# A steep-decay branch among plain units, an early load of lambda's vectors, urgent closing additions and filler ahead of the first decay

## The chip, the cores and the metric

The kernel runs on one NeuronCore of a Trainium2 chip. The metric is the device time of one execution in microseconds (us). Engine names in this text: PE is TensorE (matmuls), PEld its weight loads, DVE is VectorE, ACT is ScalarE, POOL is GpSimd, SP is SyncE, which here issues all DMAs. A "q" behind an engine's name means its instruction queue (waits, branches, register loads).

## The reference

The reference is a two-layer decoder trunk on 512 tokens of width 1024 with 16 learned meta tokens in front (528 rows). The first layer is gated linear attention in four heads with chunked decay, the second differential attention in eight heads; each has an RMSNorm before it, a SiLU gate, and a residual addition after its output projection. Cut to what matters here:

```python
def gla_branch(xn, w_in, w_gate_up, b_gate, gnorm, w_out):
    q, k, v, z, g_lr = split(xn @ w_in)
    lg = log_sigmoid(g_lr @ w_gate_up + b_gate) / GLA_TAU      # the decay's logarithm
    # per chunk, b = cumsum(lg):
    #   attn_ij = sum_d q_id k_jd exp(b_id - b_jd), j <= i
    #   o = attn v + (q exp(b)) S ;  S = exp(b_last) S + (k exp(b_last - b))^T v
    o = head_rms(o) * gnorm
    return (silu(z) * o) @ w_out

def diff_branch(xn, w_in, lam_vecs, ...):
    lv = lam_vecs                                              # four vectors of 128
    lam = exp(sum(lv[0] * lv[1])) - exp(sum(lv[2] * lv[3])) + lambda_init
    # a = softmax(q0 k0 + bias) - lam * softmax(q1 k1 + bias)
```

## The kernel before, in words

Every float32 product is made of three matmuls of split operands: a high part (rounded copy, on ACT) and a low part (the remainder, on DVE), made by `split` (L235). Activations of the first layer are held transposed in four blocks of 4 x 128 rows by 264 columns (`X`, L466).

The first layer's projections are queued as generators in a `Weaver` (class at L73, object `W`). `W.fill(us)` takes steps from the queue's head until the given sum of nominal costs is used up; `W.finish(gen)` runs the queue until that generator is done, `W.settle()` also runs what was deferred. So the order of PE's instructions is written out by the order of these calls in the source, and it is kept as written (`manual_schedule` for PE, L190). For the other engines a scheduler orders instructions at compile time from priorities, which follow the program's order, and its own estimate of when inputs are ready; `urgent` (L227) raises the priority of what a function issues. A `tc.If` block is kept together as one piece.

There are two kinds of projection unit, each 256 columns of weights wide:

- a plain unit (`plain_unit`, L713): two halves, each with two PSUM banks taken by `pb_pair` (alternately the pair bx, bx and the pair bv, by), 48 matmuls a half, 16 steps in all, each of 6 matmuls and a nominal 0.66 us. After a half, `evac` reads the banks out. The value projections and the q and k projections of head 0 are plain units.
- a `Unit` (L360): a Strassen-like scheme of seven products of 12 matmuls, each product four steps of 3 matmuls and a nominal 0.33 us. Its closing additions are in `add` (L393): they read a bank (`by`, `bv` or `bx`) and a partial sum on DVE, at L398, L400 or L402; the bank is free for PE's next product after that. `tail` (L685) multiplies finished q or k rows by their decay factor (L687). The z projections of head 0, and all projections of heads 1 to 3, are such units: two in head 0 and six in each other head.

The order around the change is this. The low-rank gate projection runs on PE with five plain steps between (L817 to L823) and is read out of its two banks (bx, bx) to `gs` (L827 to L831). Three transposes of raw input follow (L840). Then eight decays: `decay(k)` (L845) is two matmuls from `gs` (L849), three ACT steps (L850 to L852), two DVE steps (L855) and a scan along the tokens (L856) into `b_all`; after each, `W.fill(3.5)`. After the eighth, a flag is made on DVE (L871, L872): whether any chunk's decay is so steep that factors would overflow. PE sums it over partitions (L1095), DVE casts it to an integer `fi` (L1096), every engine loads it to a register (L1098) and branches (L1099) around a long block that treats steep decay; with these inputs the block is skipped. Before this branch the queue is run to the end of head 0's last plain unit (L1090), and 1.0 and 3.0 us of the first z unit follow.

Per head there then come `gla_scores` (L973), `gla_ready` (L1021) and `gla_blocks` (L1028), with filler between. At head 1, `second_layer_setup` (L883) makes the second layer's bias rows and lambda: it loads the four vectors broadcast to all partitions (L896, 256 KB), multiplies and sums them on DVE (L897, L899), and takes exponents on ACT (L900). Constants are loaded by SP at the start (L494 to L526); every DMA goes through SP's one queue in its order.

## Time and profile before

| what | value |
|---|---|
| median of 3 runs | 1049.13 us (1047.19 to 1050.68) |
| the profiled execution's own time | 1049.57 us |
| its span, first to last instruction | 1047.8 us |
| mean granted clock of PE | 0.991 |
| PE busy, 490 to 1048 us (second layer and the end) | 548.75 of 558.00 us |
| PE busy, 86 to 100 us (around the branch) | 10.36 of 14.00 us, clock 0.76 |
| DVE busy, 100 to 490 us (heads 0 to 3) | 287.15 of 390.00 us |

The span is what the profile shows; the device time has 1.8 us around it. Busy times are those of one execution. PE's rows in the order of time overlap: a matmul's shown duration is longer than the distance to the next, so costs are taken from the distance. A wait is given as the idle time in front of an instruction, with what ended it behind an arrow.

### The profile page before, as it was taken

How to read it: one execution, taken by the hardware profiler on the slowest of the kernel's cores; microseconds unless marked ns; L12 is line 12 of the kernel's file. 1: busy time of each engine (PE TensorE's matmuls, PEld its weight loads, DVE VectorE, ACT ScalarE, POOL GpSimd, SP SyncE). 2: the span in 40 equal slices, each digit the busy share in tenths (PEclk: the TensorE clock that was granted, in tenths of full speed). 3: DMA queues.
4: the chain of work that ended last, by engine and by line, in shares of the span. 5: the costliest groups of instructions: out<-in, count | busy, mean ns of one | idle time of the engine just before them, and what ended most of it. 6: DMA issues, size and time to landing. Idle time of an engine off the chain costs nothing.

```text
span 1047.8 us, 18311 instructions
## 1 busy us (share of the span) xinstructions
PE 1017.8 (97%) x7345; PEld 954.0 (91%) x7345; DVE 718.8 (69%) x1441; ACT 544.5 (52%) x1198; POOL 37.9 (4%) x68
## 2 busy tenths in 40 slices
PE   8897999999999999999999999999999999999997
PEld 7897998998899999999999898998989989889995
DVE  7886886778767887564557675755757548576675
ACT  6773764356534656536435454444544445454453
POOL 1000000000000000000000000000000000000001
PEclk9998999999999999999999999999999999999999
DMA  7222312333223312222322122232222322222212
GB/s 197 67 60 66 84 44 90 81 81 82 81 59 92 93 43 79 82 81 86 117 82 91 51 82 81 81 92 81 81 91 82 90 82 59 83 72 82 80 41 81
DMA packets 98940, 84.56 MB, mean 81 GB/s; under 512 B 5517, under 2 KB 87725, under 8 KB 98848
## 3 DMA queue, kind: packets, MB, share of 16 engines
q1 hardware_dynamic: 98848, 83.31, 26.7%
q8 instruction: 60, 0.98, 0.4%
q14 instruction: 32, 0.26, 0.1%
HBM read 83.90 MB, written 2.12 MB: 82 GB/s over the span
## 4 chain that ended last, share of the span: by engine, by line
PE 77%; DVE 7%; ACT 2%; issue 2%; DMA 2%; POOL 1%; SPq 0%; POOLq 0%; DVEq 0%; ACTq 0%
PE pp L346 32%; PE ps L325 8%; PE pp L325 7%; PE bx L355 6%; PE bx L799 4%; PE bv L355 4%; PE by L355 3%; PE bv L799 2%; PE by L799 2%; PE ps L1010 2%; PE ps L710 1%; DMA raw<-in_gla_w_in_dram 1%; DVE wl L239 1%; PE ps L1337 1%; POOL st L457 1%
## 5 line engine op out<-in xcount | busy, mean ns | idle before, releaser
L346 PE MATMUL pp<-x,wh 128*128 128x264 f32 (+1 forms) x1504 | 321.7, 323 | 0.0
L346 PEld LDWEIGHTS pp<-x,wh 128*128 128x128 f32 x1504 | 227.0, 188 | 15.5
L238 ACT ACTIVATE wh<-raw 128x512 fp32r<-128x512 f32 (+1 forms) x212 | 138.1, 680 | 119.3 <-PE pp L346 52.6
L346 PE MATMUL pp<-x,wl 128*128 128x264 f32 (+1 forms) x752 | 198.2, 319 | 0.0
L239 DVE TENSOR_TENSOR wl<-raw,wh 128x512 fp32r<-128x512 f32 (+1 forms) x212 | 156.2, 757 | 43.3 <-ACT wh L238 42.1
L346 PEld LDWEIGHTS pp<-x,wl 128*128 128x128 f32 x752 | 124.3, 188 | 10.5
L457 POOL TENSOR_TENSOR st<-st,mhalf 128x1 f32<-128x1 f32 (+1 forms) x52 | 31.1, 597 | 932.7 <-DVE st L456 932.7
L1325 ACT ACTIVATE p<-p,st 128x528 f32<-128x528 f32 (+3 forms) x64 | 36.4, 569 | 49.4 <-DVE st L1324 49.0
L325 PE MATMUL pp<-wh,x 128*128 128x256 f32 x320 | 61.3, 282 | 0.0
L355 PE MATMUL bv<-x,wh 128*128 128x264 f32 x320 | 48.5, 289 | 3.6 <-DVE t L398 1.8
L325 PEld LDWEIGHTS pp<-wh,x 128*128 128x128 f32 x320 | 51.0, 189 | 0.1
L355 PE MATMUL bx<-x,wh 128*128 128x264 f32 x320 | 48.7, 292 | 0.0
L355 PEld LDWEIGHTS bv<-x,wh 128*128 128x128 f32 x320 | 42.4, 188 | 4.9 <-DVE ks L400 2.5
L325 PE MATMUL pp<-wl,x 128*128 128x256 f32 x160 | 45.1, 282 | 0.0
L355 PEld LDWEIGHTS bx<-x,wh 128*128 128x128 f32 x320 | 43.5, 193 | 0.7 <-issue 0.6
L1322 DVE SCALAR_TENSOR_TENSOR p<-ps,qr,T 128x264 f32<-128x264 f32 (+3 forms) x80 | 36.5, 490 | 6.4 <-PE ps L325 6.4
L374 ACT ACTIVATE u<-bx 128x264 f32<-128x264 f32 x60 | 22.9, 382 | 33.1 <-PE bx L355 31.2
L239 DVE TENSOR_TENSOR aT<-ps,aT 128x512 fp32r<-128x512 f32 (+3 forms) x32 | 15.7, 489 | 31.8 <-ACT aT L238 31.6
L325 PE MATMUL ps<-k,q 128*128 128x264 f32 (+3 forms) x240 | 36.8, 294 | 0.0
L325 PEld LDWEIGHTS ps<-k,q 128*128 128x128 f32 x240 | 33.6, 188 | 0.9
L239 DVE TENSOR_TENSOR wl<-sum,wh 128x1024 fp32r<-128x1024 f32 x20 | 24.4, 1221 | 14.5 <-ACT wh L238 9.6
L325 PE MATMUL ps<-v,aT 128*128 128x256 f32 x240 | 33.9, 282 | 0.0
(399 smaller groups left out, 2209.2 us busy)
## 6 DMA issues: line engine op xcount, KB each, us to landing
raw<-in_diff_w_in_dram SPq DMA_DIRECT2D x32, 1024.0 KB
raw<-in_gla_w_in_dram SPq DMA_DIRECT2D x48, 512.0 KB
raw<-in_gla_w_out_dram SPq DMA_DIRECT2D x8, 1024.0 KB
raw<-in_diff_w_out_dram SPq DMA_DIRECT2D x8, 1024.0 KB
T<-bdr SPq DMA_DIRECT2D x8, 264.0 KB
out_dram<-z SPq DMA_DIRECT2D x8, 256.0 KB
kd<-steep SPq DMA_DIRECT2D x4, 400.0 KB
t<-steep SPq DMA_DIRECT2D x4, 264.0 KB
```

What stands on the lines that cost most here:

```text
L238: act.activation(hi, src, AF.Copy)
L239: dve.tensor_tensor(lo, src, hi.bitcast(F32), op=ALU.subtract)
L325: pe.matmul(ps, l, r, start=first and n == 0, stop=last and n == 2, **kw)
L346: pe.matmul(bank, a[:, k, :], b[k][:, n0 + i * nn:n0 + (i + 1) * nn], start=k == 0 and n == 0, stop=k == nk - 1 and n == 2)
L355: pe.matmul(bank[:, :HT], w[p][:, k * P:(k + 1) * P], x[q][:, k, :], start=first and i == 0, stop=i == len(PASSES) - 1, skip_group_check=n ...
L374: act.activation(t, self.bx[:, :HT], AF.Copy, scale=self.sc)
L457: pool.tensor_tensor(dst, dst, mhalf[:np_, :dst.shape[1]], op=ALU.pow)
L710: pe.transpose(pt[:, b * P:(b + 1) * P], vt[:, t0:t0 + n], ident)
L799: pe.matmul(banks[i][:, :HT], h.t[p][:, k, mm * P:(mm + 1) * P], s.y[q][k][:, i * HT:(i + 1) * HT], start=n == 0, stop=n == len(PASSES) - 1)
L1010: pe.matmul(o, s.kd[:, i, kc], s.qs[:, i, t0:t0 + n], start=i == 0, stop=i == 1)
L1322: dve.scalar_tensor_tensor(p[:, c0:c1], ps[:, :c1 - c0], qr[:, b:b + 1], s.T[:, c0:c1], op0=ALU.mult, op1=ALU.add)
L1325: act.activation(p[:, :nk], p[:, :nk], AF.Exp, bias=st[:, m:m + 1], accum_out=st[:, 2 + m:3 + m])
```

## The change

There are five edits.

1. The additions in `add` and the multiplication in `tail` are made `urgent`.
2. Lambda's four vectors are loaded with the first constants, transposed to one column each (512 single elements, `lv`); in `second_layer_setup` their products are two columns (`lt`), which a matmul with a matrix of ones sums over the partitions in place of the broadcast load and DVE's reduction.
3. `W.fill(4.0)` stands before the first decay; the fill after decay 0 is 2.0 in place of 3.5.
4. The flag's matmul, the branch and its fills move ahead of `W.finish(first[-1])`, `token_sums(5)` and `W.settle()`, and the second fill is 1.5 in place of 3.0. Between decay 7 and the branch PE now takes plain steps: six, two, the flag's matmul, and three; one step of the last plain unit is left behind the branch.
5. At head 1, `W.fill(4.0)` comes after `second_layer_setup` as well, not only at the other heads.

```diff
@@ -390,6 +390,7 @@
+            @urgent
             def add(i, n, bank, t, sign):
@@ -524,6 +525,9 @@
+    lv = cp.tile([P, 4], F32, name="lv")
+    with nc.allow_non_contiguous_dma(reason="four short vectors"):
+        sp.dma_start(lv, d_lam.rearrange("a p -> p a"))
     act.preload_act_table_set("natural_log_exp_and_others")
@@ -682,6 +686,7 @@
             if hd:
+                @urgent
                 def tail(i, j=j, sign=sign):
@@ -858,9 +863,10 @@
     for half in range(2):
         q_gla_z(0, heads[0], half, raw=True)
+    W.fill(4.0)
     for k in range(KT):
         decay(k)
-        W.fill(3.5)
+        W.fill(3.5 if k else 2.0)
         if 1 <= k <= 5:
             token_sums(k - 1)
@@ -892,11 +898,12 @@
-        lamb, lt = tmp()[:, :4 * P].rearrange("p (a b) -> p a b", a=4), tmp()[:, :2 * P].rearrange("p (a b) -> p a b", a=2)
-        sp.dma_start(lamb, d_lam.partition_broadcast(P))
-        dve.tensor_tensor(lt, lamb[:, 0::2, :], lamb[:, 1::2, :], op=ALU.mult)
+        lt = T(cp, [P, 2], F32, "lt")
+        dve.tensor_tensor(lt, lv[:, 0::2], lv[:, 1::2], op=ALU.mult)
+        ps = ps_tile()
+        pe.matmul(ps[:, :2], ones, lt, start=True, stop=True)
         lam2 = T(cp, [P, 2], F32, "lam2")
-        dve.tensor_reduce(lam2, lt, axis=AX.X, op=ALU.add)
+        dve.tensor_copy(lam2, ps[:, :2])
         act.activation(lam2, lam2, AF.Exp)
@@ -1087,14 +1094,11 @@
-    W.finish(first[-1])
-    token_sums(5)
-    W.settle()
     W.fill(1.0)
     pf = ps_tile()
     pe.matmul(pf[0:1, 0:1], fl[:, 1:2], one1, start=True, stop=True)
     dve.tensor_copy(fi, pf[0:1, 0:1])
-    W.fill(3.0)
+    W.fill(1.5)
     steep = nc.values_load(fi[0:1, 0:1], min_val=0, max_val=P)
     with tc.If(steep > 0):
@@ -1102,6 +1106,9 @@
         sp.dma_start(hT, hT_dr)
+    W.finish(first[-1])
+    token_sums(5)
+    W.settle()
     for hd in range(G_HEADS):
@@ -1114,8 +1121,7 @@
             if hd == 1:
                 second_layer_setup()
-            else:
-                W.fill(4.0)
+            W.fill(4.0)
```

## The prediction

> **What bounds the kernel now.** I read the page first, then who TensorE (PE) waited for, then the granted clock by stretches, then the order of time around each wait.

> ```profile
> span 1047.8 us, 18311 instructions
> PE 1017.8 (97%) x7345; PEld 954.0 (91%) x7345; DVE 718.8 (69%) x1441; ACT 544.5 (52%) x1198; POOL 37.9 (4%) x68
> ```

> PE is the bound: it is idle for 1047.8 - 1017.8 = 30.0 us, so no change of order can bring more than those 30 us, and what PE loses to a lowered clock. The list of PE's waits (total, times, longest) says where the idle time is:

> ```profile
> PE bv L355 <- PEq L1099: 3.6, 1, 3.6
> PE bv L355 <- DVE t L398: 1.8, 1, 1.8
> PE ps L849 <- DVE a L831: 1.7, 1, 1.7
> PE bv L355 <- DVE ks L400: 1.7, 2, 0.9
> PE bx L355 <- DVE ks L698: 1.6, 1, 1.6
> PE ps L849 <- ACT hT L565: 0.7, 1, 0.7
> PE by L355 <- DVE t L398: 0.4, 1, 0.4
> ```

> All seven lie in the first layer, and each is touched by one edit: L1099 is the branch on `steep`, L849 the first decay, the wait of 1.8 stands behind lambda's load, L698 is the closing of the last plain unit, and L400 and the last L398 are additions in `add`. Together 11.5 us. The second cost shows in the busy times by stretches (the column PEclk is the granted clock):

> ```profile
> core 0: us, PE busy (x) PEld busy (x) DVE busy (x) ACT busy (x) POOL busy (x), PEclk, DMA share, GB/s
> 35.00:38.40 3.40, 3.40 (x18) 3.40 (x17) 3.40 (x7) 2.82 (x6) 0.00 (x0) 0.50 0.00 0
> 93.00:99.80 6.80, 5.45 (x26) 5.21 (x27) 2.48 (x5) 0.39 (x1) 0.00 (x0) 0.50 0.03 8
> 168.10:171.50 3.40, 3.40 (x18) 2.94 (x17) 2.12 (x5) 2.40 (x5) 0.00 (x0) 0.50 0.00 0
> ```

> After each of the three larger stalls PE runs at half clock: 3.40, 5.45 and 3.40 us of work, of which half is lost, so 1.7, 2.7 and 1.7 us on top of the waits. (The start-up, ahead of the change, has one more such stretch.) The unit of all that follows is one matmul of 264 columns, from the chain of waits:

> ```profile
> 103.92 1.46 PE bv L355 x12
> ```

> 1.46 / 12 = 0.122 us. A step of a plain unit is 6 of them (0.73 us, counted as 0.66 by the filler), a step of a `Unit` 3 (0.37 us, counted as 0.33).

> **The change part by part. First decay.**

> ```profile
> 30.76 0.66 PE L559 MATMUL ps<-ident,v 128*128 128x128 f32 x4 [0.39 <-ACT hT L565]
> 33.72 0.42 DVE L831 TENSOR_TENSOR a<-bx,a 16x264 fp32r<-16x264 f32 x1
> 34.20 0.39 PE L849 MATMUL ps<-a,z 128*128 128x264 f32 x1 [1.72 <-DVE a L831]
> ```

> PE ends the transposes at 31.42 and then has only the first decay, whose input DVE finishes at 34.14 (33.72 + 0.42): 0.7 and 1.7 us of waiting, 2.4 in all. `W.fill(4.0)` issues seven plain steps there (six count 3.96, not yet 4.0), 5.1 us, so PE arrives at 36.5 and finds everything ready: -2.4. One thing can come late: five steps were issued before, so the fourth of the seven begins the value unit's second half, in the bank pair that the gate projection's evacuation (L831) still reads. PE gets there at 31.4 + 3 x 0.73 = 33.6, up to 0.6 before 34.2. I take -2.2 (-2.4 to -1.8). The half clock of 35.0 to 38.4 goes with the gap: -1.7 (-1.7 to 0, if the clock falls elsewhere). The smaller fill after decay 0 (four steps for six) means that all later decays stand at about their old times, and PE is five plain steps (5 x 0.73 = 3.65 us) further in the units.

> [...]

> **The branch.** Three waits are to be priced. First, the flag. PE's one-column matmul L1095 (before, long after the flag) now follows decay 7 after 6 + 2 plain steps.

> ```profile
> 70.20 0.40 PE L849 MATMUL ps<-a,z 128*128 128x264 f32 x2
> 73.52 0.74 ACT L852 ACTIVATE t<-t,ones 128x528 f32<-128x528 f32 x1
> 76.05 0.76 DVE L855 SCALAR_TENSOR_TENSOR t<-ps,t 128x264 f32<-128x264 f32 x2
> 77.07 1.25 DVE L856 TENSOR_TENSOR_SCAN keep<-c,t 128x528 f32<-128x528 f32 x1
> 79.30 0.14 DVE L872 TENSOR_SCALAR fl<-fl 128x1 f32<-128x1 f32 x1
> ```

> From decay 7's first matmul to the flag it took 79.44 - 70.20 = 9.2 us, while PE now offers 0.25 + 8 x 0.73 = 6.1. If that stays, PE stands 3.1 us at the flag. But of the 9.2 us, 1.8 lie between the end of L852 (74.26) and L855, and 1.0 between the end of the scan (78.32) and L872, while DVE did weight splits and closings, which now come five plain steps earlier. Without these two the chain is 6.4: 0.3 over PE's 6.1. Bounds 0 and 3.1; I take +1.0, nearer to the row without queues, since the work in those queues is moved ahead of it.

> Second, the branch itself.

> ```profile
> L1099 ACTq COMPARE_BRANCH  x1: 50/50/50, 91.2 to 91.2; - x1
> L1099 PEldq COMPARE_BRANCH  x1: 5214/5214/5214, 89.0 to 89.0; - x1
> L1099 ACTq EVENT_SEMAPHORE  x1: 17/17/17, 94.8 to 94.8; - x1
> ```

> These are the branch's line (durations in ns, then when it ran); in the order of time around it:

> ```profile
> 86.65 0.19 PE L1095 MATMUL ps<-ones,fl 128*1 128x1 f32 x2
> 87.79 0.14 DVE L1096 CAST fi<-ps 1x1 int32<-1x1 f32 x1
> 94.35 1.00 PE L355 MATMUL bv<-x,wl 128*128 128x264 f32 x3 [3.65 <-PEq L1099]
> ```

> From L1095 to the first matmul behind the branch: 94.35 - 86.65 = 7.7 us, of which PE's branch takes 5.2. It is covered by what the filler put between: ten steps of 3 matmuls, 3.7 us, and the flag's own 0.2; the rest is the 3.65 of idle time. The move does not take the branch away, and `W.fill(1.5)` in plain steps is three, 18 matmuls, 2.2 us: the cover shrinks, and the stall is 7.7 - 2.4 = 5.3 if nothing else changes. Shorter: the cast stood 0.95 behind its matmul (87.79 against 86.84) and PE will be waiting, so it may follow in 0.3; and ACT was away only 94.8 - 91.2 = 3.6 us at the same branch, where PE took 5.2. With both, 3.0. I take 4.3, the middle, since no row says what the 5.2 us depend on: +0.65 (-0.65 to +1.65).

> [...]

> Third, the wait behind the last plain unit (1.64, L698). It now comes after the branch, with one plain step left, and DVE has nothing in front: the bank is free after one L698 (0.42) and some 0.3 of handing over, so 0.7: -0.9 (-1.6 to 0). Behind the branch the unit's other needs, the second weight pair and `token_sums(5)`, have 16 steps of 0.37 before PE uses them. The half clock after the branch (2.7 us) I leave as it is; one window of 3.4 us more or less is +1.7 or -1.7. Sum of the branch: +0.75 (-4.0 to +6.5).

> **Lambda.**

> ```profile
> 36.16 0.16 DVE L903 TENSOR_SCALAR dgs<-dg_sb 128x2 f32<-128x2 f32 x1
> 161.78 0.36 SPq L896 DMA_DIRECT2D t<-in_diff_lam_dram  x1
> 165.31 0.43 DVE L897 TENSOR_TENSOR t<-t 128x256 f32<-128x256 f32 x1 [3.89 <-DMA t<-in_diff_lam_dram]
> 167.12 1.34 PE L355 MATMUL bv<-x,wh 128*128 128x264 f32 x8 [1.80 <-DVE t L398]
> ```

> DVE stood 3.9 us at L897 for a transfer issued 3.5 us earlier; the closings queued behind it held PE's bank, 1.8 us, and the clock fell, 1.7. With `lv` loaded at the start this goes. Late next: the new matmul waits for `lt` in PE's fixed order. L903 is written in the same function and needs only an early load, and DVE ran it at 36.16; `lt` is its like, so no wait. The matmul itself costs about what L1095 does, 0.2, with its copy on DVE unseen: +0.3 taken. In all -1.8 - 1.7 + 0.3 = -3.2 (-3.5 to 0). The earlier load is one more issue on SP:

> ```profile
> 21.02 1.03 SPq L526 DMA_DIRECT2D dg_sb<-in_diff_gnorm_dram  x1
> 23.35 0.99 SPq L254 DMA_DIRECT2D raw<-in_gla_w_in_dram  x2
> ```

> At 1.0 us it fits between 22.05 and 23.35; uncovered it would delay a weight load by that 1.0, whose splits come far later. The extra `W.fill(4.0)` at head 1 only moves steps from the filler's end to ahead of the scores: 0.

> **Urgent closings.**

> ```profile
> 185.99 0.43 DVE L400 TENSOR_TENSOR t<-bv,u 128x264 f32<-128x264 f32 x1 [0.61 <-PE bv L355]
> 269.01 0.68 DVE L239 TENSOR_TENSOR y<-t,y 128x512 fp32r<-128x512 f32 x1
> 269.61 0.42 DVE L400 TENSOR_TENSOR ks<-bv,u 128x264 f32<-128x264 f32 x1
> ```

> At 269.6 the addition stood behind a split of 0.68, which it now passes: 0.6 of that wait's 0.85 goes, twice, and perhaps the 0.4 of `by`. At 186 DVE itself waited for PE, so there is nothing to pass. I take -1.2 (-2.1 to +1.0, if a split that is passed comes late).

> **Sum.** -2.2 - 1.7 + 0.75 - 3.2 - 1.2 = -7.55. The profiled execution took 1049.57 us, 1.77 over its span and 0.44 over the median of 1049.13; 1049.57 - 7.55 = 1042.0, or 1041.6 against the median. I say 1042.

> **The rivals.** (a) DVE sets the flag. If the flag comes at 79.4 as before, whatever PE does, PE's flag matmul is at 79.5, the first matmul behind the branch at 87.2; one plain step (0.73), 0.7 of waiting and the 15 unit steps that lay before the branch (1 in `finish`, 4 and 10 in the two fills; 5.5) bring PE to 94.1, where it stood at 94.35. The whole gain of the first decay is then spent at the branch, and 1049.6 - 0.25 - 3.2 - 1.2 = 1045 remains. For it: DVE's queue set the flag's time before. Against it: DVE was not full there:

> ```profile
> 36.50:79.40 42.90, 42.90 (x350) 42.84 (x350) 35.74 (x56) 32.81 (x65) 0.00 (x0) 0.98 0.25 67
> ```

> 35.74 of 42.90 us busy leaves 7 us to bring the flag forward.

> (b) Slower: the urgent closings push weight splits back. The 20 units of the layer (two of head 0, six of each other head) have 80 additions of 0.43 us; where one passes a split that PE needs next, PE waits that long. Without the 1.2 the other terms give -6.35, so it decides from (6.35 + 3.1) / 0.43 = 22 such waits; at 25 the time is 1049.6 - 6.35 + 10.75 = 1054. Against it: no wait of PE on a weight split is among the seven rows, which are the larger ones of this layer.

> (c) The clock falls anyway, a little later, as its windows fall otherwise: 1042 + 3.4 = 1045.4. For it: what idle share lowers it no row says, and the three runs lie 3.5 us apart (1047.19 to 1050.68), about two such losses.

> (d) Lambda's edit does not do what it says: `lt` is put behind the bias copies, and PE waits at the new matmul in place of the old stall: 1042 + 3.2 = 1045.

> **How the numbers follow.** Forecast 0.55, (a) 0.22, (b) 0.07, (c) 0.10, (d) 0.06. About 0.3%, 3.1 us, is what a measurement of this kernel can tell from no change, so faster means below 1046.0. The forecast is there nearly always, (a), (c) and (d) in six of ten: 0.53 + 0.6 x 0.38 = 0.76, and I put 0.73 because the branch's upper bound alone is 5.75 over what I took. Slower is (b) and the sum of bad bounds, 0.08; the rest, 0.19, is the same. All good bounds together lie 6.1 below the sum taken (-13.7 against -7.55); the range goes down by somewhat over half of that, to 1038.5, and up to 1047.5, past (a), (c) and (d).

> **What would show it.** Right: no wait at L849 and a clock of 1.0 at 35 to 38; L897 without a DMA before it and no half clock at 168; a wait at L1099's branch of 3 to 5.3, and one of 0 to 3 at the flag's matmul on DVE's flag; the waits on `ks` in `add` below 0.4 each. Wrong: a wait at the flag over 3, waits on weight splits in heads 1 to 3, or any new wait of PE over 1 us in the second layer, which the change does not touch.

## The result and the profile after

The changed kernel takes 1041.4 us (median of 6 runs, 1040.07 to 1042.38) where the kernel before took 1049.4 (6 runs, 1047.19 to 1050.76): a ratio of 0.9922, 95% interval 0.9909 to 0.9936, so 8.0 us less. The forecast was 1042.0. The profiled execution took 1040.18 us.

The edits add lines, so the same place has another number in each kernel: the branch is L1099 before and L1103 after, the closing of a plain unit L698 and L703, the first decay L849 and L854. L1017 is a matmul of `gla_ready` that waits for a split of the values, L1080 a transpose in `rows` that waits for ACT's scaled copy of a head's output. The head of the page after:

```profile
span 1038.4 us, 18321 instructions
PE 1012.7 (98%) x7347; PEld 949.6 (91%) x7347; DVE 718.8 (69%) x1441; ACT 543.2 (52%) x1198; POOL 38.5 (4%) x68
```

PE is idle for 25.7 us instead of 30.0: 4.3 of the 9.4 us between the two profiled executions. The other 5.1 are in PE's busy time, 1017.8 against 1012.7, with two short matmul instructions more: the same work at a higher clock. The list of PE's waits after (total, times, longest):

```profile
PE bx L355 <- DVE ks L703: 2.3, 1, 2.3
PE bx L726 <- PEq L1103: 2.0, 1, 2.0
PE ps L1080 <- ACT t L1058: 1.9, 5, 0.5
...
PE ps L1099 <- DVE fl L878: 1.2, 1, 1.2
...
PE ps L1017 <- DVE v L239: 1.0, 1, 1.0
...
PE bx L726 <- DVE a L836: 0.6, 1, 0.6
...
PE ps L715 <- DVE cm L335: 0.5, 1, 0.5
```

Of the seven rows that the prediction showed, the first decay's two are down to the 0.6 at L726, lambda's 1.8 and the three additions in `add` (1.7 and 0.4) are gone, and the branch is still there, in three parts: the flag 1.2, the branch 2.0, the closing behind it 2.3. Four rows are new or larger (L1080, L1017, L715, and L1099). The prediction calls its seven the larger ones of the first layer; one more of that size stands in the same list of the kernel before, a wait of the output projection for an addition in `add`:

```profile
PE bv L799 <- DVE t L400: 1.9, 3, 0.6
```

It is 1.2 after (L804). Busy times by stretches, the column PEclk being the granted clock:

```profile
core 0: us, PE busy (x) PEld busy (x) DVE busy (x) ACT busy (x) POOL busy (x), PEclk, DMA share, GB/s
16.00:32.00 16.00, 13.96 (x102) 12.07 (x103) 15.68 (x22) 11.12 (x20) 0.02 (x1) 1.00 0.53 106
35.00:38.40 3.40, 3.40 (x31) 3.39 (x30) 3.37 (x7) 3.16 (x7) 0.00 (x0) 1.00 0.00 0
80.08:83.49 3.41, 0.97 (x6) 0.78 (x6) 1.22 (x3) 0.98 (x2) 0.00 (x0) 1.00 0.06 17
83.49:90.31 6.82, 5.47 (x24) 5.34 (x24) 4.13 (x8) 1.65 (x3) 0.00 (x0) 0.50 0.55 155
168.10:171.50 3.40, 3.40 (x27) 2.97 (x26) 2.63 (x7) 1.32 (x4) 0.00 (x0) 1.00 0.35 137
```

The half-clock stretches at 35 and at 168 are gone: 31 and 27 matmuls lie there where 18 lay. The one behind the branch has stayed (5.47 us of work against 5.45). The one at the start-up (21 to 25 us before) is absent too, which no edit reaches; the runs below show that it comes and goes. Three stretches of 1.7 us are the 5.1 us of busy time. Not all of this is the change. The stretch at 168 stood in this one profile: the five kernels below that keep lambda's load have PE wait for it too, by 1.3 to 2.5 us, and none of them shows half clock behind it. So 3.4 of the 9.4 us between these two executions may be chance, and the change is better read from the medians, 8.0. Over all runs the mean granted clock is 0.9928 after and 0.9906 to 0.9919 in the four series of the kernel before, which is 0.9 to 2.3 us of 1049; the larger part of the 8.0 us is no matter of the clock.

The order of time around the branch (PE's rows and DVE's, put in order):

```profile
77.01 0.19 PE L1099 MATMUL ps<-ones,fl 128*1 128x1 f32 x2 [1.16 <-DVE fl L878]
81.60 0.97 PE L726 MATMUL bx<-x,wl 128*128 128x264 f32 x6 [2.04 <-PEq L1103]
82.27 0.43 DVE L676 TENSOR_SCALAR t<-keep 128x528 f32<-128x528 f32 x1 [2.28 <-DVEq L1103]
83.22 1.22 DVE L239 TENSOR_TENSOR wl<-raw,wh 128x1024 fp32r<-128x1024 f32 x1
84.36 0.77 DVE L703 SCALAR_TENSOR_TENSOR ks<-bx,t 128x264 f32<-128x264 f32 x2
84.84 2.13 PE L355 MATMUL bx<-x,a11h 128*128 128x264 f32 x8 [2.27 <-DVE ks L703]
```

PE is back from the branch at 81.60 and has done the unit's last step at about 82.5; DVE is back at 82.27, and then clips the decay (L676) and splits a weight (L239, 1.22) ahead of the closing that PE waits for.

### The profile page after: what moved, and what is told of

Same layout as the page of the kernel before. It is cut to its first block, busy times and chain, and to the rows that moved or that the text cites. A ratio compares the mean times of both kernels' runs of the same rounds, so it can differ in the third digit from the quotient of the medians.

```text
span 1038.4 us, 18321 instructions
## 1 busy us (share of the span) xinstructions
PE 1012.7 (98%) x7347; PEld 949.6 (91%) x7347; DVE 718.8 (69%) x1441; ACT 543.2 (52%) x1198; POOL 38.5 (4%) x68
## 3 DMA queue, kind: packets, MB, share of 16 engines
HBM read 83.64 MB, written 2.12 MB: 83 GB/s over the span
## 4 chain that ended last, share of the span: by engine, by line
PE 81%; DVE 6%; ACT 2%; issue 1%; POOL 1%; DMA 1%; POOLq 0%; SPq 0%; DVEq 0%
PE pp L346 33%; PE ps L325 8%; PE pp L325 7%; PE bx L355 7%; PE bv L355 5%; PE bx L804 4%; PE by L355 4%; PE bv L804 2%; PE by L804 2%; PE ps L1017 2%; DVE wl L239 1%; PE ps L715 1%; POOL st L458 1%; PE ps L1343 1%; PE ps L1080 1%
## 5 line engine op out<-in xcount | busy, mean ns | idle before, releaser
L239 DVE TENSOR_TENSOR wl<-raw,wh 128x512 fp32r<-128x512 f32 (+1 forms) x212 | 156.2, 757 | 43.3 <-ACT wh L238 42.5
L355 PE MATMUL bx<-x,wh 128*128 128x264 f32 x320 | 47.8, 287 | 0.0
L355 PE MATMUL bv<-x,wh 128*128 128x264 f32 x320 | 47.6, 287 | 0.0
L355 PEld LDWEIGHTS bx<-x,wh 128*128 128x128 f32 x320 | 42.3, 188 | 0.5 <-issue 0.4
L355 PEld LDWEIGHTS bv<-x,wh 128*128 128x128 f32 x320 | 42.4, 189 | 0.2
L239 DVE TENSOR_TENSOR aT<-ps,aT 128x512 fp32r<-128x512 f32 (+3 forms) x32 | 15.7, 489 | 31.8 <-ACT aT L238 31.6
L239 DVE TENSOR_TENSOR wl<-sum,wh 128x1024 fp32r<-128x1024 f32 x20 | 24.4, 1221 | 14.1 <-ACT wh L238 12.5
```

What stands on the lines that cost most here:

```text
L239: dve.tensor_tensor(lo, src, hi.bitcast(F32), op=ALU.subtract)
L355: pe.matmul(bank[:, :HT], w[p][:, k * P:(k + 1) * P], x[q][:, k, :], start=first and i == 0, stop=i == len(PASSES) - 1, skip_group_check=n ...
```

## The experiments

All are timed against the kernel before on the same chip; ratios are of those runs, with their 95% intervals, and the microseconds won are worked out from the ratios. The theory to be tested was the prediction's sum, five edits with prices of their own; the rival, that the edits work only through each other, or that the gain comes from somewhere that the sum does not name. So first each edit was put alone on the kernel before, then pairs, then what was disputed was measured by itself.

**Lambda alone.** Edit 2 on the kernel before, nothing else:

```diff
+        sp.dma_start(lv, d_lam.rearrange("a p -> p a"))
...
-        sp.dma_start(lamb, d_lam.partition_broadcast(P))
+        dve.tensor_tensor(lt, lv[:, 0::2], lv[:, 1::2], op=ALU.mult)
+        pe.matmul(ps[:, :2], ones, lt, start=True, stop=True)
```

> The kernel before with lambda's edit alone. Theory 1 (the terms of the sum hold one by one): no wait of DVE on lambda's load, no wait of PE behind it, no half clock near 168 us, -3.0 to -3.5 us. Rival (what is saved there comes back at the next wait of the same head, since DVE's later work sets PE's pace): the wait moves, -1.5 us or less.

Measured: 1047.99 us (12 runs), ratio 0.9987 (0.9972 to 1.0002), 1.4 us. The load's wait and the half clock at 168 are gone, though the mean clock of the twelve runs is no higher than that of the kernel before (0.9906 against 0.9919). And the list of waits has a new row, and the order of time shows what it is:

```profile
PE ps L996 <- DVE t L896: 1.4, 1, 1.4
```

```profile
158.89 0.89 DVE L896 COPY t<-ps 8x328 f32<-8x328 f32 x2
...
159.43 1.83 PE L996 MATMUL ps<-qs,ks 128*128 128x128 f32 x14 [1.42 <-DVE t L896]
```

The new matmul takes one more PSUM tile of the rotation of four, so that head 1's scores come to the tile in which the bias rows still stand; DVE copies those (L896) only after the urgent steps of the scores. Most of lambda's wait has come back one step later.

**The filler in head 1 alone, and with lambda.** Edit 5 on the kernel before, then edits 2 and 5:

```diff
-            else:
-                W.fill(4.0)
+            W.fill(4.0)
```

> The kernel before with only the 4 us of filler that the change adds in head 1 behind the second layer's setup. The lambda edit alone gave 1.6 us, with this filler 6.1. Theory: the filler moves head 1's scores 4 us back on PE, so that DVE and ACT have done head 1's key closings, weight splits and copies when PE asks for them (in the pair's profile the waits for the second product's bank, 0.4 and 0.7 us, and for ACT's copies, 0.5 us, are gone as well as the scores' 1.4 us), and it is worth 1 to 3 us by itself, with lambda's 1.8 us wait left in place (ratio 0.9971 to 0.9990). Rival, the price of the prediction: nothing by itself (1.0000 +- 0.0008); it matters only as cover for what the lambda edit adds.

Measured: 1048.59 us (12 runs), ratio 0.9979 (0.9966 to 0.9992): 2.2 us for an edit that I had priced at nothing. The transfer of lambda's vectors still holds PE, longer than before in the profiled execution (2.5 us in place of 1.8), but no half clock follows it there. Where the 2.2 us come from this profile does not show: two waits of 0.6 us in head 1 are gone, but another, ahead of head 2's blocks, is 1.6 in place of 0.4.

> The kernel before with the lambda edit and, as the change has it, 4 us of filler also in head 1 behind the second layer's setup. Theory: the filler, which I had priced at nothing, is what covers the scores' wait for DVE's bias copies (1.4 us with the lambda edit alone); then there is no wait over 0.5 us between 150 and 175 us, no half clock there, and the kernel takes 3.0 to 4.0 us less than before (ratio 0.9962 to 0.9972). Rival: the wait at the scores is only put off, and lambda with the filler is worth what lambda alone was, 1 to 2 us (ratio about 0.9987).

Measured: 1043.7 us (6 runs), ratio 0.9942 (0.9924 to 0.9959): 6.1 us, three quarters of the whole change and more than the 3.0 to 4.0 expected. The row of PE's stage, with the waits gone and the clock up:

```profile
150.00:175.00 25.00, 24.83 (x199) 23.19 (x197) 19.42 (x42) 14.58 (x29) 0.55 (x1) 1.00 0.25 81
```

PE idles 0.17 us in those 25. The filler's four microseconds let DVE copy the bias rows before the scores ask for their tile, so that lambda's new wait of 1.4 us does not arise, and the wait on an addition in `Unit` (`bv`, L799) is 1.2 in place of 1.9. Against the profile before, the rows that vanish are lambda's wait and half clock (3.5), these 0.7, 0.5 of the waits for ACT's copies and 0.4 of `by`: some 5 us; the interval reaches from 4.3 to 8.0 us.

The profiles allow a test that does not hang on single rows: the time that PE takes from the first product of head 0's blocks to the first of head 3's (the matmul of `s.am` in `gla_blocks`). It is 307.2 us before, 306.6 to 308.1 in the five other kernels that keep the load, the one with the filler alone among them (306.9), 304.2 with lambda alone and 300.8 with lambda and filler. So the pair's gain is there in the profiles, 6.4 us, and 2.4 of it lie behind the first product of head 1's blocks, which no term of these two edits reaches. One wait there goes with the load: ahead of head 2's blocks PE waits 0.4 to 1.8 us for an addition in all six kernels that keep it, and in none of the eight without it is this wait over 0.25 us.

**The first decay alone, the branch alone, and both.** Edit 3; edit 4; the two together:

```diff
+    W.fill(4.0)
     for k in range(KT):
         decay(k)
-        W.fill(3.5)
+        W.fill(3.5 if k else 2.0)
```

> The kernel before with the filler at the first decay alone (4.0 before decay 0, 2.0 after it). Theory 1: PE's wait at the first decay falls from 2.4 to about 0.6 us and the half clock at 35 us goes, -2.5 to -3.5 us. Rival (DVE sets the pace up to the flag, so that PE only comes earlier to the last plain unit's closing): the wait on that closing (1.6 us before) grows by what was saved, 0 to -1 us.

Measured: 1046.75 us (12 runs), ratio 0.9974 (0.9962 to 0.9986), 2.7 us of the 3.9 forecast. The wait at the first decay fell to 0.5 us and the clock stayed up, but at the branch, which then still stood behind the plain units, some was given back (3.4 us at half clock, from 82.25, also came anew):

```profile
PE bv L355 <- PEq L1100: 4.0, 1, 4.0
PE bx L355 <- DVE ks L698: 2.3, 1, 2.3
```

```diff
-    W.finish(first[-1])
-    token_sums(5)
-    W.settle()
...
     with tc.If(steep > 0):
...
+    W.finish(first[-1])
+    token_sums(5)
+    W.settle()
```

> The kernel before with the move of the branch alone. Theory 1 (the move pays only by what it meets): PE waits 1 to 3 us at the flag and 2 to 5 us at the branch, and about 2 us at the last plain unit's closing, in sum 0 to +3 us against the 5.3 us of before. Rival (the branch hides better among plain steps): the waits at flag, branch and closing are together under 4 us, -1.5 us or better.

Measured: 1049.30 us (12 runs), ratio 1.0003 (0.9991 to 1.0014). The closing's wait shrank to 0.9, near the 0.7 of the prediction, and the branch's to 0.8, but PE stood at the flag, and 1.5 us more behind the branch, for which the list names no cause:

```profile
PE ps L1092 <- DVE fl L872: 3.6, 1, 3.6
...
PE bx L721 <- issue: 1.5, 1, 1.5
```

This is rival (a) of the prediction: without the filler ahead of the decays DVE sets the flag, at about its old time (80.0 us, 79.4 before), and what the move gains is spent there.

> The kernel before with the filler at the first decay and the branch move together, nothing else. Alone they gave 2.8 us and 0.3 us. Theory: each mends what the other spoils. The filler brings the flag early enough that PE waits 1 to 2 us for it instead of 3.6, and the branch runs with no weight load in flight, so PE's branch takes 3.0 to 3.6 us instead of 5.5; the stage from 31 to 92 us has one half-clock stretch instead of two, and the pair gives 4.5 to 5.5 us (ratio 0.9948 to 0.9957). Rival: they add up, 3.1 us (ratio 0.9970), and the excess of the whole change over its parts comes from elsewhere.

Measured: 1047.0 us (10 runs), ratio 0.9975 (0.9960 to 0.9990), 2.6 us. The flag's wait is down to 1.2 and the branch's to 2.1, as the theory said, but the pair is worth what the filler alone is worth: the closing behind the branch waits 1.8, and half clock follows. The theory's 4.5 to 5.5 us fell; the two edits add up, as its rival said.

**The urgent marks alone, and the change without them.** Edit 1:

```diff
+            @urgent
             def add(i, n, bank, t, sign):
...
+                @urgent
                 def tail(i, j=j, sign=sign):
```

> The kernel before with the urgent additions and tails alone. Theory 1: the waits on the additions of ks and of by (1.7 and 0.4 us) go and nothing takes their place, -1.2 us. Rival, from the profile after: they go, but the transposes wait for ACT's scaled rows (1.9 us in place of 0.7) and a cross product waits for a weight split (1.0 us), so that it comes to 0, between -0.7 and +0.7 us.

Measured: 1049.63 us (12 runs), ratio 1.0004 (0.9992 to 1.0015). The waits on `ks` in `add` are gone, and others stand in their place:

```profile
PE ps L1075 <- ACT t L1053: 3.1, 7, 0.9
...
PE ps L1012 <- DVE v L239: 1.0, 1, 1.0
```

The first was 0.7 in the kernel before, the second not in the list: scaled copies of a head's output (the expectation below calls them score copies) and a split of the values, which the additions now pass.

> The changed kernel without the two urgent marks (closing additions and closing products stand where they did in DVE's queue). Alone on the kernel before, the marks were worth nothing (ratio 1.0004). Theory: here too; PE waits again about 2.1 us for the key products' closing additions and about 1.2 us less for ACT's score copies, 1.0 less for the weight split and 0.5 less elsewhere, and the time is within 1 us of the changed kernel, 1040.4 to 1042.4. Rival: the marks are worth the 1.2 us that the prediction gave them, or more because other edits took their counterpart away: 1042.6 or more.

Measured: 1040.28 us (4 runs), ratio 0.9918 (0.9896 to 0.9940), against 0.9922 with the marks. Both ways round they are worth nothing that can be measured. With this the parts add up: lambda with its filler 5.8 per mille, decay with branch 2.5, together 8.3; the change without the marks 8.2.

**A transfer under the branch.** In all other profiles PE's branch took 4.5 to 6.1 us where a weight load was under way (in one for its first microsecond only) and 3.3 to 3.7 where none was, but the branch also stood elsewhere in the code. So a transfer of no use was put under the changed kernel's branch:

```diff
+    scr = T(dp, [P, KT, L], F32, "scr")
+    sp.dma_start(scr, b_all)
```

> The changed kernel with one transfer more, of no use to the result: the whole decay tensor, 128 x 4224 elements (2.16 MB), to a scratch tensor in DRAM, issued when the last scan is done, so that it is in flight while the engines take the branch. No engine waits for it. Theory: the branch costs PE 3.3 us when no data transfer is in flight and 4.5 to 5.5 us when one is (in the four runs in which a weight load was under way it took 4.5 to 5.5, in the two in which none was, 3.3 and 3.6); so PE's branch goes to 4.5 us or more, PE idles 1.2 to 2.5 us longer at it, and the time grows by 1.2 to 3 us. Rival: what differs between those runs is the place of the code, not the transfers; the branch stays at 3.3 +- 0.3 us and the time within 0.7 us of the changed kernel.

Measured: 1045.56 us (9 runs), ratio 0.9960 (0.9946 to 0.9974), 4 us more than the changed kernel, where 1.2 to 3 were expected. The branch's line in the changed kernel, and then in this one (duration in ns):

```profile
L1103 PEldq COMPARE_BRANCH  x1: 3332/3332/3332, 78.1 to 78.1; - x1
```

```profile
L1105 PEldq COMPARE_BRANCH  x1: 6652/6652/6652, 79.9 to 79.9; - x1
```

The transfer ran at 416 GB/s under the branch, PE's wait there was 6.0 us in place of 2.0, and the half clock lasted one stretch longer:

```profile
78.00:83.20 5.20, 2.55 (x20) 2.30 (x20) 4.91 (x9) 2.74 (x3) 0.00 (x0) 0.95 0.99 416
82.70:92.94 10.24, 4.53 (x19) 4.26 (x20) 3.31 (x7) 1.27 (x2) 0.00 (x0) 0.50 0.29 88
```

So the time of PE's branch goes with what else the core's DMA engines carry: 3.3 us with 14 GB/s moved from 78.0 to 83.2 us, 6.7 us with 416. The likely reason, an inference from the traces, is that the branch waits for code to be fetched by these engines: the page of the changed kernel lists a queue of instruction transfers among the DMA queues.

```profile
q8 instruction: 59, 0.97, 0.4%
```

The times of its packets agree with this reason. In the changed kernel one packet of 16 KB on this queue begins 1.0 us after PE's branch and has landed at 80.06, 1.4 us before the branch ends. With the useless transfer it begins 4.2 us after the branch, 3.2 later, and the branch ends 3.3 us later, again 1.4 us behind the landing. In all fourteen profiles such a packet lies under PE's branch, which ends 1.4 to 2.3 us after the last has landed. The 1.5 us without a named cause, behind the branch of the kernel with edit 4 alone, end at 88.19, again 1.4 us after such a packet. The traces also show a second difference between the old place and the new: under the branch at its old place there are two such packets in all six profiles, at its new place one in all eight. In the kernel with edit 3 alone the weight load was over some 1 us after the branch began, and the branch still took 5.5 us. So what was saved at the new place (5.2 to 3.3 us) need not be the weight load's alone; how much is the second packet's no run separates.

**The closing behind the branch.** The factor of the last half unit is made ahead of the branch, and the plain units' closings go first in DVE's queue:

```diff
+    heads[0].early()        # ready[1] = factor_of(1, -1.0), in a tile of its own
     W.fill(1.5)
     steep = nc.values_load(...)
...
+                @urgent
                 def evac(...):
-                    e = factor_of(i, sign)
+                    e = ready[i] if i in ready else factor_of(i, sign)
```

> The changed kernel, with the decay factor of the last plain unit's second half (the clip on DVE and the exponential on ACT) written ahead of the branch into a tile of its own, and the plain units' closings marked urgent. Theory: PE's 2.3 us wait behind the branch is for a closing in front of which DVE, back from the branch 0.5 to 0.7 us after PE, first clips (0.43 us) and splits a weight (1.22 us); with the factor ready and the closing ahead of the split the wait falls to 0.8 to 1.3 us, PE idles less than half of every 3.41 us stretch there, one of the two half-clock stretches or both go, and the time falls by 1 to 4 us, to 1037.4 to 1040.4. Rival: the wait is set by the products themselves (the last six matmuls run only behind the branch, until 82.6 us); the closing's 0.77 us and the way back leave 2 us or more, and the time is within 0.7 us of the changed kernel.

Measured: 1040.48 us (6 runs), ratio 0.9903 (0.9885 to 0.9921). The wait fell from 2.3 to 0.7 us, with the closing now ahead of the split:

```profile
PE bx L355 <- DVE ks L708: 0.7, 1, 0.7
```

That is the mechanism, shown. The half clock did not go: the stretch with the branch's own wait is still more than half idle (below). The ratio is the lowest of all runs, but its interval overlaps that of the change, so the 1 to 4 us expected are not shown.

**Work for the clock.** Two attempts to keep PE busy around the branch. First ten matmuls behind it:

```diff
+    idle = ps_tile()
+    for _ in range(10):
+        pe.matmul(idle[:, :P], ones, ones, start=True, stop=True)
     W.finish(first[-1])
```

> The changed kernel with ten matmuls of ones by ones (128 x 128, result unused) right behind the branch, ahead of the last six products of the plain unit: 1.3 to 2.1 us of work for PE of no use, laid into its wait for the closing. In ten profiles every 3.41 us stretch of the clock in which PE idled 1.70 us or more was followed by a stretch at half clock, and none at full clock with 1.64 us or less. Theory: it is this share of idle time that lowers the clock; the added work cuts the idle time of the stretch before 83.5 us from 2.4 to about 1.5 us, the half-clock stretches behind the branch go, and the time falls by 1.5 to 3.4 us although PE has more to do: 1038.0 to 1039.9. Rival: the clock falls for another reason (the branch itself, or the sum of waits over a longer stretch); the half-clock stretches stay and the added work costs 0 to 0.5 us: 1041.4 to 1041.9.

Measured: 1042.68 us (6 runs), ratio 0.9927 (0.9908 to 0.9947), above the 1038.0 to 1039.9 of the theory; the half clock stayed. But this run does not decide, since its edit missed: the ten waited at the branch themselves (2.8 us), came when the clock was down already, and took 4.6 us. Then, with the early factor kept, twelve products as PE's last work before the branch:

```diff
+    for _ in range(12):
+        pe.matmul(idle[:, :512], xs[1][:, :P], xs[0][:, :512], start=True, stop=True)
     steep = nc.values_load(...)
```

> The changed kernel with the early factor and the urgent closings of the run before, and twelve products of 512 columns (result unused) written as PE's last work before it loads the flag and branches. A product of 264 columns takes 0.12 us, so these are estimated at 0.23 us each, 2.7 us in all; PE's sequencer goes on ahead of the array by ten to thirteen products (the branch starts 1.45 us before the array runs dry), so that most of this work lies under the branch. Theory: the half-clock stretches behind the branch follow from the 1.96 us in which PE idles at the branch within one 3.41 us stretch. With the queue filled that idle time falls to 0.3 to 1.0 us, no stretch has 1.7 us of idle time, the clock stays up behind the branch (6.8 us at half clock become none, 3.4 us gained), the added work costs 2.7 less the 1.0 to 1.7 us of idle time that it replaces, and the time is 1 to 3 us below that of the run before, a ratio of 0.987 to 0.989. Rival: the clock falls whatever PE does around the branch; the half-clock stretches stay, the added work costs 1 to 2 us net, ratio 0.991 to 0.992.

Measured: 1041.59 us (6 runs), ratio 0.9928 (0.9908 to 0.9949). The stretches around the branch, with the early factor alone:

```profile
79.60:83.02 3.42, 1.46 (x12) 1.28 (x11) 1.79 (x2) 1.40 (x2) 0.00 (x0) 1.00 0.05 14
83.02:89.84 6.82, 6.08 (x28) 5.78 (x27) 4.41 (x9) 1.19 (x3) 0.00 (x0) 0.50 0.34 90
```

and with the twelve products:

```profile
79.00:82.42 3.42, 3.42 (x24) 3.07 (x23) 3.39 (x4) 1.92 (x2) 0.00 (x0) 1.00 0.04 10
82.42:85.83 3.41, 2.04 (x11) 1.32 (x9) 0.98 (x3) 0.00 (x0) 0.00 (x0) 1.00 0.04 12
85.83:92.66 6.83, 6.51 (x55) 6.34 (x56) 6.04 (x13) 1.54 (x3) 0.00 (x0) 1.00 0.55 149
```

The clock stays at 1.00: 55 matmuls where 28 lay. The branch's wait is 0.7. So in the profiled execution the theory of the clock holds and its rival falls. Its price does not: the ratio was to be 0.987 to 0.989, and the rival's 0.991 to 0.992 lies in the interval. The twelve took 3.0 us, and replaced 1.3 us of idle time at the branch. No gain in time is shown, nor a loss.

## Why the prediction was right, and where its steps were wrong

The total is right, by terms of which some were wrong in opposite directions; that it came within 0.6 us is in part luck: lambda with its filler, priced at 3.2, gave 6.1, the urgent marks, priced at 1.2, nothing, and decay with branch 2.6 for 3.15.

- **First decay, -2.2 and -1.7.** Right in kind: the wait went from 2.4 to 0.6 and the clock at 35 to 38 is 1.00. The bank that L831 still reads cost 0.6, the bound named for it, so -1.8. The clock's 1.7 is at the low end: of the six profiles that keep the old order here two show one half-clock stretch at this place and four show two, and none of the other eight shows any. Alone the edit gave 2.7 of the 3.9 us, and with the branch's move 2.6.
- **The branch, +0.75.** In the two profiles the three waits were 5.3 before (3.65 and 1.64) and are 5.5 after: +0.2, and the half clock behind them is unchanged, as forecast. The flag, +1.0, measured 1.2. The other two were wrong and cancel. "I take 4.3, the middle, since no row says what the 5.2 us depend on": it was 2.0, below the lower bound of 3.0. Two things that the branch's time goes with are absent at the new place: the weight load that ran under it before (134 GB/s from 89.6 to 93.0 us, 17 GB/s from 80.1 to 83.5 now), and one of two packets of code. The useless transfer, put under the branch at the new place, makes the wait 6.0. "DVE has nothing in front", so 0.7: it was 2.3, over the bound of 1.6. The move put a step with all its followers behind the branch, and DVE comes back from it 0.7 us after PE, with the clip and a split of 1.22 us ahead of the closing; with these out of the way it is 0.7 indeed.
- **Lambda, -3.2.** The load's wait and the half clock went, and `lt` was done at 35.2 us, like its neighbour, as forecast:

```profile
L902 DVE TENSOR_TENSOR lt<-lv x1: 156/156/156, 35.2 to 35.2; 128x2 f32<-128x2 f32 x1
```

  But alone this gave 1.4 us. The 1.7 us for the clock were a chance of one execution (none of the five other profiles with the load has half clock there), and the scores waited 1.4. Rival (d) was close: the bias copies do hold PE, through the PSUM tile that the new matmul uses up, not through `lt`.
- **"The extra `W.fill(4.0)` at head 1 only moves steps from the filler's end to ahead of the scores: 0."** The step that failed. Alone it gave 2.2 us (0.8 to 3.6), which its profile does not show; with lambda 6.1 where lambda alone gave 1.4, and this the profiles do show (300.8 us against 304.2 from head 0's blocks to head 3's). Moving steps ahead of the scores is not free of effect: it sets how late everything else may be that the scores need.
- **Urgent closings, -1.2.** Nothing. Between the change without and with them, the waits on `ks` (1.7 us) go, and others come for ACT's copies (0.6 to 1.9), a split that was passed (1.0) and L715 (0.5): rival (b)'s mechanism, on a small scale. Most of what comes sits in head 3: from its scores to its blocks PE takes 48.7 to 48.8 us in the six profiles with the marks and 46.8 to 46.9 in the eight without. The row of L799, an addition in `add` too, the marks alone leave at 1.9. (The 0.4 of `by` is gone without the marks too.)
- **The sum.** Decay and branch add up as the sum has it (2.7, nothing, 2.6 together). Lambda and its filler share a stage and seem not to (1.4 and 2.2 alone, 6.1 together), though the intervals of the three leave room for a plain sum.

Of the signs named beforehand, those for the clock, for L897, for the flag and for `ks` in `add` came; the branch's 3 to 5.3 did not. No wait on a weight split arose in heads 1 to 3, and none in the second layer.

What stays open: why the filler alone gives 2.2 us, through what the lambda edit shortens the waits ahead of head 2's blocks, how the branch's time divides between the load under it and its code, and whether the early factor is worth anything in time.

## What to carry to other kernels

A filler that seems only to move work is a deadline for everything behind it: price it by the waits that it covers, and test an edit together with the cover that it came with. When a branch is moved, look at what is in flight under it, data and code, and at what every engine must still do behind it before the first engine can go on. A higher priority for what PE waits for now is worth nothing where what it passes is what PE waits for next. And count a lowered clock as saved only if it stands in more than one profile.

## What the runs showed of the hardware

```profile
340.05:343.47 3.42, 1.72 (x13) 1.44 (x12) 3.42 (x8) 0.70 (x2) 0.00 (x0) 1.00 0.00 0
343.47:346.88 3.41, 3.41 (x18) 3.41 (x17) 2.86 (x6) 3.04 (x7) 0.54 (x1) 0.50 0.21 51
```

```profile
83.51:86.92 3.41, 1.76 (x15) 1.55 (x14) 3.41 (x6) 0.61 (x2) 0.00 (x0) 1.00 0.00 0
86.92:90.34 3.42, 3.42 (x30) 3.24 (x29) 3.10 (x8) 1.34 (x3) 0.00 (x0) 1.00 0.67 186
```

Ahead of 28 us, where matmuls stand apart and each is shown longer than it holds the array (in rows 0.28 us, with the next 0.12 behind it), half clock came after stretches shown with only 0.9 to 1.3 us of idle time, and not after all of these; so the bound is one of shown busy time, and of long rows of matmuls. A wait of 1.8 us can halve the clock of the next 3.41 us or leave it, by where the grid cuts it: lambda's 1.8 did before, a 2.5 in its place did not with head 1's filler alone. Several waits within one stretch count together: in the stretch from 80.08 after, 1.5 us of the branch's and 0.9 of the closing's, each less than the 1.65 that were not enough in the second case above. Ahead of 343.47, in the first case above, 1.70 us of idle time in a stretch were enough.

**This is much of the scatter.** Around the gate projection at the start-up, which no edit reaches, a profile has no, one or two half-clock stretches (clock 1.00, 0.89 and 0.79 from 16 to 32 us, after, before, and with decay and branch), 1.7 us each; the runs of one kernel lie 2 to 8 us apart. The granted clock recorded for each run goes with its time: among 35 runs of the kernel before, the correlation is -0.81.

**The branch cost 3.3 to 3.7 us on PE without a data transfer in flight, in seven profiles, and 4.5 to 6.7 with one, in seven.** Six of the latter also have two packets of code under the branch in place of one; the seventh, with the useless transfer, has one. DVE at the same branch was away from 79.98 to 82.27 in the profile after, 2.3 us.
